# Squares and roots pinned to their written order on ScalarE around a pooling layer, and eps taken over a squared factor instead of a product after the root

## The chip, the cores and the metric

The kernel runs on one core of a Trainium2 chip. The metric is device time in microseconds (us), from launch to end, lower is better; the figure for the kernel before is the median of three runs. The engines are TensorE (PE), VectorE (DVE), ScalarE (ACT), GpSimd (POOL) and SyncE (SP, which issues the DMAs of weights).

## The reference, cut to what matters

512 tokens of width 1024 go through two blocks in float32. The second block has two layers. Layer 0 is attention and a SwiGLU FFN; layer 1 is a pooling mixer and a SwiGLU FFN. Every part is normed before and after:

```
rmsnorm(x, g) = x * rsqrt(mean(x*x) + eps) * g
h = h + rmsnorm(mixer(rmsnorm(h, g0)), g1)
h = h + rmsnorm(swiglu(rmsnorm(h, g2)), g3)
```

The pooling mixer takes, in four groups of 256 channels, the trailing mean over 2, 4, 8 or 16 tokens minus the token, a 256x256 map for each group, and a scale for each channel. `eps` is 1e-6.

## The kernel before, in words

Float32 products are made of three matmuls on operands split into a high part and a rest: weights `raw` come by DMA (512 KB each, from SP), ACT copies the high part `wh`, DVE subtracts for the rest `wl`. All tiles of this kind share one set of 37 buffers, so a load starts when a buffer comes free. The four token tiles of 128 are numbered 0 to 3; `XT[i]` is the residual of tile i, tokens on partitions, in two halves of 512 channels.

Operations go through a helper, so the trace gives all of them line 113. They are followed here by tile names.

**Norms.** The FFN's input is not normed before its matmuls. `Raw.put` (lines 1019 to 1026) transposes the plain residual and writes it, times the gain, to `H`; the tokens' factor `ra` = 1/sqrt(mean square + eps) is found beside it by `rstd_col` (999 to 1006) in `to_raw` (1072 to 1075), spread over partitions by PE and copied to `rsb` by ACT (`factors`, 1028 to 1031). The gate's output is multiplied by `rsb` ahead of SiLU. The up part is not multiplied, so the FFN's output lacks a factor `ra` for each token. The norm after it makes this good (`PostT.close`, 1061 to 1070): the root is taken of ss * ra*ra/D + eps, and its reciprocal is multiplied by `ra`. `factors` keeps ra*ra/D in `ra2` for that.

**The closing norm of a token tile.** `PostT.square` (1056 to 1059) squares each half `mg` on ACT with a sum over the row, and POOL multiplies the half by the gain. `close` adds the two sums on DVE (`sd`), takes the root on ACT (`sd`), the reciprocal on DVE (`rs`), and updates both halves of `XT` on DVE; then ACT squares both halves of `XT` for the next norm. In the second FFN `to_pool` (1708 to 1715) takes the next root and writes the scaled tokens `xs`, one half on ACT and one on DVE.

**Order of the work around the pooling layer** (1748 to 1784). `f2.last(h, j)` ends the FFN of layer 0 for two token tiles and one half of the channels; `band` multiplies `xs` by banded matrices, for two tiles at a time, and ACT and DVE write the result to `H`; `pool_step(i)` is the 256x256 maps of tile i, its closing norm and the `Raw.put` for the next FFN; `heads` are gate and up steps of an FFN on the first 256 tokens, written early so that PE has work. As written: `f2.last` for tiles 0 and 1, and the first half of the channels for tiles 2 and 3; the first band; pool steps 0 and 1; `f2.last` for tiles 2 and 3; two gate and up steps of the last FFN, whose evacuation is put off; the second band; the evacuation; pool steps 2 and 3; three more gate and up steps; the rest of the last FFN.

This is the order in which the code is written. The Tile framework schedules it: on each engine an instruction may be moved ahead of earlier ones that are not ready by its estimate. `keep` stops this for one instruction: it must come behind the instruction written just before it on its engine. In the kernel before, `keep` is on the roots of `rstd_col` and on the SiLUs put off. The squares have none. PSUM has four banks `mm`, two `ax` and two `st`; a gate and up step uses two of `mm`.

Of the kernel before, what the change touches and what calls it, by code (L numbers as in the profile page):

```python
# [11 lines left out]
AF = mybir.ActivationFunctionType  # L12
OP = mybir.AluOpType
# [5 lines left out]
D = 1024  # L19
# [12 lines left out]
EPS = 1e-6  # L32
# [88 lines left out]
def body(ctx: ExitStack, tc: tile.TileContext, I: dict, out, dbg=None):  # L121
# [12 lines left out]
    def A(name, dt=F32):  # L134
        tag, bufs = TAGS.get(name, ("m", NB))
        return ar.tile([P, 2, S], dt, tag=tag, name=name, bufs=bufs)
# [4 lines left out]
    def SQ():  # L141
        return tp.tile([P, S], F32, tag="sq", name="sq", bufs=BS)
# [4 lines left out]
    def small(w, name):  # L147
        return tp.tile([P, w], F32, tag=f"sm{w}", name=name, bufs=6)

    def MM():  # L150
        return ps.tile([P, S], F32, tag="mm", name="mm", bufs=4)
# [7 lines left out]
    def act(o, i, f=AF.Identity, **kw):  # L159
        ins = SC.activation(o, i, f, **kw)  # L160
        if f in KEEPF and not SC.on:
            tc.keep_in_program_order(ins)
        return ins

    def keep(ins):

        if KEEP:
            tc.keep_in_program_order(ins)

    def stt(o, a, s, b, op0, op1):  # L170
        return V.scalar_tensor_tensor(o, a, s, b, op0=op0, op1=op1)

    def tt(o, a, b, op):
        return V.tensor_tensor(o, a, b, op=op)

    def ts(o, a, s, op, s2=None, op2=None):
        if op2 is None:
            return V.tensor_scalar(o, a, s, None, op0=op)
        return V.tensor_scalar(o, a, s, s2, op0=op, op1=op2)
# [7 lines left out]
    def columns(name, w, t=None):  # L187

        if t is None:
            t = cp.tile([P, w], F32, name=name)  # L190
        used = [0]

        def f(n):
            used[0] += n
            return t[:, used[0] - n:used[0]]
        return f

    C = columns("fixed", 1576)

    ident, ones, blk = C(P), C(P), C(P)  # L200
    epsc = C(1)
# [33 lines left out]
    for i in range(4):  # L235
        a = A("xtok")
# [47 lines left out]
    class Weights:  # L284


        def __init__(self, look):
            self.look, self.deep = look, 1
            self.specs, self.loaded, self.ready, self.done = [], [], [], 0
            self.pool = False  # L290
            self.hp = 0
# [179 lines left out]
    def mm_tok(o, op, slabs, i, k0=0, first=True, last=True):  # L471
        lst = list(wk(slabs))
        ks_ = k0 if isinstance(k0, tuple) else range(k0, k0 + len(lst))
        for n, (k, (wh, wl)) in enumerate(zip(ks_, lst)):
            th, tl = op.tok(k, i)
            TE.matmul(o, lhsT=th, rhs=wh, start=(first and n == 0), stop=False)
            TE.matmul(o, lhsT=tl, rhs=wh, start=False, stop=False)
            TE.matmul(o, lhsT=th, rhs=wl, start=False, stop=(last and n == len(lst) - 1))
# [20 lines left out]
    def spread(rs, n, bank=ST):  # L499
        psb = bank()  # L500
        for i in range(n // P):
            TE.matmul(psb[:, i * P:(i + 1) * P], lhsT=rs[:, i:i + 1].to_broadcast([P, P]), rhs=ident, start=True, stop=True)
        return psb[:, :n]
# [454 lines left out]
    def heads(n, **kw):  # L958

        for _ in range(min(n, len(nx["head"]))):  # L960
            nx["head"].popleft()(**kw)

    def run(seq, n_of, step, close):

        left = {h: n_of for h in HALVES}
        cl = {}
        for m, c0, c1 in seq:
            step(m, c0, c1)
            for h in HALVES:
                if c0 <= h[0] and h[1] <= c1:  # L970
                    left[h] -= 1
                    if left[h] == 0:
                        cl[h] = close(*h)
                        if h == HALVES[0]:
                            next(cl[h])
                            next(cl[h])
                        else:
                            closing(cl[HALVES[0]], cl[h])
# [17 lines left out]
            return cache[m]  # L996
        return get

    def rstd_col(ss, out, ra=None):

        sd = small(4, "sd")
        tt(sd[:, :1], ss[:, 0:1], ss[:, 1:2], OP.add)
        keep(act(sd[:, 1:2], sd[:, :1], AF.Sqrt, scale=1.0 / D if ra is None else ra[1], bias=epsc))
        V.reciprocal(out, sd[:, 1:2])
        if ra is not None:
            tt(out, out, ra[0], OP.mult)

    XT = []

    class Raw:  # L1010


        def __init__(self, g, name):
            self.g = g
            self.ra = C(4)
            self.ra2 = C(4)
            self.rsb = tp.tile([P, S], F32, tag="rsb", name="rsb", bufs=1)

        def put(self, i):
# [8 lines left out]
        def factors(self, i):  # L1028
            a = self.ra[:, i:i + 1]
            act(self.rsb[:, i * P:(i + 1) * P], spread(a, P), AF.Copy)  # L1030
            stt(self.ra2[:, i:i + 1], a, 1.0 / D, a, OP.mult, OP.mult)

        def of(self, i):
            return self.ra[:, i:i + 1], self.ra2[:, i:i + 1]

    def row_of(src):

# [4 lines left out]
    class PostT:  # L1042
# [12 lines left out]

        def square(self, i, j):
            mv = self.m(i, j)
            act(SQ(), mv, AF.Square, accum_out=self.ss[:, i, j:j + 1])
            (G if TG[j] else V).tensor_tensor(mv, mv, self.gb[:, j], op=OP.mult)

        def close(self, i, last=False):
            rs = small(4, "rs")[:, :1]
            rstd_col(self.ss[:, i], rs, self.ra and self.ra.of(i))
            for j in range(2):
                x = XT[i][:, j]
                stt(x, self.m(i, j), rs, x, OP.mult, OP.add)
                if last:
                    nc.sync.dma_start(out[0, i * P:(i + 1) * P, j * S:(j + 1) * S], x)
                else:
                    act(SQ(), x, AF.Square, accum_out=self.ss[:, i, 2 + j:3 + j])  # L1070

        def to_raw(self, i):
            self.raw.put(i)
            rstd_col(self.ss[:, i, 2:], self.raw.ra[:, i:i + 1])
            self.raw.factors(i)

    posts = []

    def gate_up_step(op, hid, get, raw=None):
        def f(m, c0, c1, late=None):  # L1080
            n = c1 - c0
            sl = get(m)
            if hid.t[m] is None:
                hid.t[m] = A("hid", F32R)
            pg, pu = MM(), MM()
            mm_tile(pg[:, :n], op, sl[:1], c0, c1)
            mm_tile(pu[:, :n], op, sl[1:], c0, c1)

            def evac():
                t = T("silu")  # L1090
                if raw is None:
                    a = act(t[:, :n], pg[:, :n], AF.Silu)
                else:
                    tt(t[:, :n], pg[:, :n], raw.rsb[:, c0:c1], OP.mult)
                    a = act(t[:, :n], t[:, :n], AF.Silu)
                if late is not None or KEEPS:
                    keep(a)
                tt(t[:, :n], t[:, :n], pu[:, :n], OP.mult)
                hid.put(m, t[:, :n], c0, c1)
            if late is None:  # L1100
                evac()
            else:
                late.append(evac)
        return f
# [550 lines left out]
    def dump_tok(name):  # L1655
        if dbg is not None and name in dbg:
            for i in range(4):
                for k in range(KD):
                    nc.sync.dma_start(dbg[name][:, k, i * P:(i + 1) * P].rearrange("c t -> t c"), XT[i][:, k // 4, k % 4 * P:(k % 4 + 1) * P])
# [48 lines left out]
    def to_pool(i):  # L1708
        x_ = A("xs")
        xs.append(x_)  # L1710
        p = pf["p"]
        rs = small(4, "rs")[:, :1]
        rstd_col(p.ss[:, i, 2:], rs)
        act(x_[:, 0], XT[i][:, 0], AF.Copy, scale=rs)
        ts(x_[:, 1], XT[i][:, 1], rs, OP.mult)
# [19 lines left out]
    def pool_step(i):  # L1735
        psb, pp = pf["psb"], pf["pp"]
        for j in range(2):
            (wh, wl, _), = getp(j)
            o = MM()
            for e in range(2):  # L1740
                g = 2 * j + e
                mm_tok(o[:, e * HS:(e + 1) * HS], HO, [(wh[:, 2 * e:2 * e + 2], wl[:, 2 * e:2 * e + 2], 2)], i, 2 * g)
            tt(pp.m(i, j), o, psb[:, j], OP.mult)
            pp.square(i, j)
        pp.close(i)
        pp.to_raw(i)
# [10 lines left out]
    def after2(i):  # L1757
        f2.p.close(i)
        to_pool(i)
    f2.last(0, 0)  # L1760
    f2.last(0, 1, after2)
    f2.last(1, 0)
    band(*HALVES[0])
    pool_step(0)
    pool_step(1)
    f2.last(1, 1, after2)
    f3 = FfnT(HO, raw1, HEAD3)
    W.ahead(6)
# [7 lines left out]
        drain(e() for e in late)  # L1776
    pool_step(2)
    pool_step(3)
    heads(HEAD3)
    dump_tok("ha1")  # L1780
    f3.front(lambda: PostT(gnorm(1, 3), None, raw1))
# [24 lines left out]
```

## Time and profile before

| | us |
|---|---|
| median of 3 runs | 1663.76 |
| lowest, highest | 1662.12, 1664.29 |
| profiled execution | 1662.05 |
| its span, first to last instruction | 1660.3 |
| PE busy in the span | 1626.7 (98%) |
| DVE busy | 879.6 (53%) |
| ACT busy | 681.0 (41%) |
| POOL busy | 129.3 (8%) |

The span is what the trace covers; the time of an execution is a little more than its span. Times in the rows below are from the span's start. The pooling layer and the ends of its neighbours lie between about 1228 and 1330 us.

### The profile page before, as it was taken

What the parts mean: (1) busy time and instruction counts of PE and PEld (TensorE: products, weight loads), DVE (VectorE), ACT (ScalarE), POOL (GpSimd) and SP (SyncE); (2) the same over time, 40 slices, a digit from 0 to 9 for tenths busy, and PEclk for the clock granted to TensorE, in tenths of its full rate; (3) what the DMA queues carried; (4) which work ended last, traced back from release to release, by engine and by line L of the source; (5) the groups of instructions that cost most, each with busy time, mean ns of one, the idle gap of its engine ahead of it and who ended that gap; (6) DMA issues with size and microseconds to landing.
All of it is one profiled execution on the core that took longest, in us unless ns stands there. A gap on an engine that the chain in (4) does not pass through costs nothing.

```text
span 1660.3 us, 21934 instructions
## 1 busy us (share of the span) xinstructions
PE 1626.7 (98%) x8733; PEld 1355.0 (82%) x8733; DVE 879.6 (53%) x1644; ACT 681.0 (41%) x1231; POOL 129.3 (8%) x144
## 2 busy tenths in 40 slices
PE   7998999999999999999999999999998999999998
PEld 5886698888888998777778888888888998888886
DVE  4799583444433584778857344423257734432244
ACT  4585352322123455455658223313237823322232
POOL 0452000000000011101011000000022100000002
PEclk9999999999999999999999999999999999999999
DMA  9635434445452333301144133234221533232511
GB/s 306 180 113 209 161 99 117 136 132 173 146 139 80 95 79 79 90 26 52 39 134 108 51 101 89 83 107 140 77 89 54 138 89 102 75 108 92 144 38 51
DMA packets 245167, 179.53 MB, mean 108 GB/s; under 512 B 20688, under 2 KB 220224, under 8 KB 245064
## 3 DMA queue, kind: packets, MB, share of 16 engines
q1 hardware_dynamic: 240520, 176.99, 36.2%
q10 hardware_dynamic: 4544, 1.14, 0.4%
q8 instruction: 68, 1.11, 0.3%
q14 instruction: 35, 0.29, 0.1%
HBM read 175.99 MB, written 2.11 MB: 107 GB/s over the span
## 4 chain that ended last, share of the span: by engine, by line
PE 86%; DVE 4%; ACT 1%; issue 0%; DMA 0%; DVEq 0%; ACTq 0%
PE mm L113 80%; PE ax L113 3%; PE st L113 3%; DVE pw L113 1%; ACT sq L113 0%; DMA raw<-in_ffn_w_gate_dram 0%; DVE wl L113 0%; ACT pw L113 0%; DVE XT L113 0%; DVE H L113 0%; DVE sq L113 0%; DVE mg L113 0%; DVE pt L113 0%; DVE lg L113 0%; DVE fk L113 0%
## 5 line engine op out<-in xcount | busy, mean ns | idle before, releaser
L113 PE MATMUL mm<-H,wh 128*128 128x512 f32 (+1 forms) x3168 | 869.8, 360 | 7.4 <-ACT H L113 2.4
L113 PEld LDWEIGHTS mm<-H,wh 128*128 128x128 f32 x3168 | 563.7, 189 | 106.6 <-issue 8.7
L113 PE MATMUL mm<-H,wl 128*128 128x512 f32 (+1 forms) x1584 | 567.9, 359 | 0.0
L113 DVE TENSOR_TENSOR wl<-raw,wh 128x1024 fp32r<-128x1024 f32 (+1 forms) x257 | 309.7, 1218 | 232.9 <-ACT wh L113 219.8
L113 PEld LDWEIGHTS mm<-H,wl 128*128 128x128 f32 x1584 | 299.3, 189 | 46.8 <-issue 3.4
L113 ACT ACTIVATE wh<-raw 128x1024 fp32r<-128x1024 f32 (+1 forms) x257 | 261.4, 1040 | 132.6 <-PE mm L113 66.6
L113 PE MATMUL mm<-wh,hid 128*128 128x512 f32 x704 | 217.4, 389 | 0.0
L113 DVE TENSOR_TENSOR silu<-silu,mm 128x512 f32<-128x512 f32 (+1 forms) x77 | 47.0, 611 | 252.2 <-PE mm L113 248.2
L113 PEld LDWEIGHTS mm<-wh,hid 128*128 128x128 f32 x704 | 132.1, 188 | 27.1
L113 ACT ACTIVATE hid<-silu 128x512 fp32r<-128x512 f32 (+1 forms) x77 | 43.9, 570 | 254.7 <-DVE silu L113 254.7
L113 PE MATMUL mm<-wl,hid 128*128 128x512 f32 x352 | 137.3, 390 | 0.0
L113 PE MATMUL mm<-hid,wh 128*128 128x512 f32 (+1 forms) x464 | 117.1, 341 | 0.0
L113 PEld LDWEIGHTS mm<-hid,wh 128*128 128x128 f32 x464 | 80.2, 190 | 10.7 <-issue 1.2
L113 POOL TENSOR_TENSOR mg<-mg,gb 128x512 f32<-128x512 f32 x32 | 44.2, 1388 | 464.7 <-ACT sq L113 459.1
L113 ACT ACTIVATE silu<-silu 128x512 f32<-128x512 f32 (+1 forms) x52 | 29.3, 565 | 124.7 <-DVE silu L113 124.7
L113 PE MATMUL mm<-hid,wl 128*128 128x512 f32 (+1 forms) x232 | 79.0, 341 | 0.0
L113 PEld LDWEIGHTS mm<-wl,hid 128*128 128x128 f32 x352 | 66.1, 188 | 14.1 <-DVE wl L113 0.3
L113 DVE TENSOR_TENSOR silu<-mm,rsb 128x512 f32<-128x512 f32 (+1 forms) x52 | 31.6, 608 | 73.3 <-PE mm L113 72.6
L113 PE MATMUL mm<-wh,H 128*128 128x512 f32 (+2 forms) x256 | 66.0, 345 | 2.8 <-ACT wh L113 1.6
L113 DVE TENSOR_TENSOR hid<-silu,hid 128x512 fp32r<-128x512 f32 (+1 forms) x77 | 47.3, 614 | 32.5 <-ACT hid L113 32.5
L113 POOL TENSOR_TENSOR cv<-cv,tap 128x488 f32<-128x488 f32 (+12 forms) x40 | 52.5, 1345 | 88.1 <-ACT cv L113 71.1
L113 DVE SCALAR_TENSOR_TENSOR ax<-glu,fixed,ax 128x511 f32<-128x511 f32 (+21 forms) x76 | 51.4, 732 | 0.0
(271 smaller groups left out, 1582.8 us busy)
## 6 DMA issues: line engine op xcount, KB each, us to landing
adaw<-in_ada_w_dram SPq DMA_DIRECT2D x48, 512.0 KB
raw<-in_w_ffn_in_dram SPq DMA_DIRECT2D x44, 512.0 KB
raw<-in_ffn_w_gate_dram SPq DMA_DIRECT2D x44, 512.0 KB
raw<-in_ffn_w_up_dram SPq DMA_DIRECT2D x44, 512.0 KB
raw<-in_ffn_w_down_dram SPq DMA_DIRECT2D x44, 512.0 KB
raw<-in_w_in_dram SPq DMA_DIRECT2D x16, 512.0 KB
adaw<-in_ada_f_w_dram SPq DMA_DIRECT2D x16, 512.0 KB
raw<-in_attn_w_in_dram SPq DMA_DIRECT2D x16, 512.0 KB
```

The costliest lines, as they stand in the source:

```text
L113: ins = f(*a, **k)
```

## The change

The root of the closing norm now has `eps` / (ra*ra) as its bias and the constant 1/D as its scale: the factor `ra` cancels, and the product after the reciprocal goes. The earlier root `sd` is 1/ra, so `eps` times its square is computed in `to_raw` by one `scalar_tensor_tensor`, behind `factors`, which no longer computes `ra2`. This holds for both FFNs of the second block: eight closing norms, four token tiles each.

Between the second FFN's end and pool step 3 (`kept`), the squares in `PostT.square` and in `PostT.close` are kept in their written order as well.

```
--- before.py
+++ after.py
@@ -996,14 +996,13 @@
             return cache[m]
         return get
 
-    def rstd_col(ss, out, ra=None):
+    def rstd_col(ss, out, bias=None):
 
         sd = small(4, "sd")
         tt(sd[:, :1], ss[:, 0:1], ss[:, 1:2], OP.add)
-        keep(act(sd[:, 1:2], sd[:, :1], AF.Sqrt, scale=1.0 / D if ra is None else ra[1], bias=epsc))
+        keep(act(sd[:, 1:2], sd[:, :1], AF.Sqrt, scale=1.0 / D, bias=epsc if bias is None else bias))
         V.reciprocal(out, sd[:, 1:2])
-        if ra is not None:
-            tt(out, out, ra[0], OP.mult)
+        return sd[:, 1:2]
 
     XT = []
 
@@ -1013,7 +1012,7 @@
         def __init__(self, g, name):
             self.g = g
             self.ra = C(4)
-            self.ra2 = C(4)
+            self.eps = C(4)
             self.rsb = tp.tile([P, S], F32, tag="rsb", name="rsb", bufs=1)
 
         def put(self, i):
@@ -1028,10 +1027,9 @@
         def factors(self, i):
             a = self.ra[:, i:i + 1]
             act(self.rsb[:, i * P:(i + 1) * P], spread(a, P), AF.Copy)
-            stt(self.ra2[:, i:i + 1], a, 1.0 / D, a, OP.mult, OP.mult)
 
         def of(self, i):
-            return self.ra[:, i:i + 1], self.ra2[:, i:i + 1]
+            return self.eps[:, i:i + 1]
 
     def row_of(src):
 
@@ -1055,7 +1053,9 @@
 
         def square(self, i, j):
             mv = self.m(i, j)
-            act(SQ(), mv, AF.Square, accum_out=self.ss[:, i, j:j + 1])
+            a = act(SQ(), mv, AF.Square, accum_out=self.ss[:, i, j:j + 1])
+            if kept[0]:
+                keep(a)
             (G if TG[j] else V).tensor_tensor(mv, mv, self.gb[:, j], op=OP.mult)
 
         def close(self, i, last=False):
@@ -1067,14 +1067,18 @@
                 if last:
                     nc.sync.dma_start(out[0, i * P:(i + 1) * P, j * S:(j + 1) * S], x)
                 else:
-                    act(SQ(), x, AF.Square, accum_out=self.ss[:, i, 2 + j:3 + j])
+                    a = act(SQ(), x, AF.Square, accum_out=self.ss[:, i, 2 + j:3 + j])
+                    if kept[0]:
+                        keep(a)
 
         def to_raw(self, i):
             self.raw.put(i)
-            rstd_col(self.ss[:, i, 2:], self.raw.ra[:, i:i + 1])
+            sd = rstd_col(self.ss[:, i, 2:], self.raw.ra[:, i:i + 1])
             self.raw.factors(i)
+            stt(self.raw.eps[:, i:i + 1], sd, EPS, sd, OP.mult, OP.mult)
 
     posts = []
+    kept = [False]
 
     def gate_up_step(op, hid, get, raw=None):
         def f(m, c0, c1, late=None):
@@ -1757,6 +1761,7 @@
     def after2(i):
         f2.p.close(i)
         to_pool(i)
+    kept[0] = True
     f2.last(0, 0)
     f2.last(0, 1, after2)
     f2.last(1, 0)
@@ -1776,6 +1781,7 @@
         drain(e() for e in late)
     pool_step(2)
     pool_step(3)
+    kept[0] = False
     heads(HEAD3)
     dump_tok("ha1")
     f3.front(lambda: PostT(gnorm(1, 3), None, raw1))
```

## Rows read from the trace of the kernel before

**Rows 1.** The first line of the page.
```profile
span 1660.3 us, 21934 instructions
```

**Rows 2.** Busy time by stretch, from the pooling layer to the end; columns: the stretch in us from the span's start and its length, then for PE, PE's weight loads, DVE, ACT and POOL the busy us and the number of instructions, then TensorE's granted clock, the busy share of the DMA engines and GB/s.
```profile
1228.00:1248.40 20.40, 20.40 (x91) 16.60 (x90) 15.09 (x31) 10.50 (x21) 5.93 (x4) 1.00 0.29 90
1248.40:1266.00 17.60, 13.25 (x89) 11.63 (x88) 14.30 (x24) 12.11 (x28) 6.05 (x4) 1.00 0.44 120
1266.00:1300.00 34.00, 34.00 (x246) 32.14 (x245) 25.52 (x65) 25.67 (x68) 5.14 (x4) 1.00 0.39 102
1300.00:1326.00 26.00, 26.00 (x220) 25.91 (x219) 20.63 (x48) 24.67 (x54) 5.93 (x4) 1.00 0.35 91
1326.00:1648.00 322.00, 322.00 (x1509) 270.41 (x1508) 112.98 (x137) 88.85 (x122) 7.90 (x6) 1.00 0.29 87
1648.00:1660.30 12.30, 4.82 (x22) 3.65 (x20) 5.80 (x12) 2.22 (x6) 2.55 (x2) 0.89 0.22 85
```

**Rows 3.** PE's waits between 1225 and 1335 us; columns: who waited for whom, us in total, times, the longest.
```profile
PE ax L113 <- ACT xs L113: 2.0, 1, 2.0
PE ax L113 <- DVE XT L113: 1.1, 1, 1.1
PE mm L113 <- DVE H L113: 0.9, 1, 0.9
PE mm L113 <- ACT H L113: 0.3, 1, 0.3
```

**Rows 4.** ACT's instructions in order of time, 1237 to 1253 us, some of them; columns: start, duration in us, engine, line, operation, out<-in, count, and in brackets the idle time before and what ended it.
```profile
1237.94 0.63 ACT L113 ACTIVATE sq<-mg 128x512 f32<-128x512 f32 x1 [2.58 <-DVE mg L113]
...
1238.57 1.04 ACT L113 ACTIVATE wh<-raw 128x1024 fp32r<-128x1024 f32 x1
1239.63 1.28 ACT L113 ACT_TABLE_LOAD   x1
...
1244.16 0.62 ACT L113 ACTIVATE sq<-mg 128x512 f32<-128x512 f32 x1
...
1245.36 0.72 ACT L113 ACTIVATE xs<-XT,rs 128x512 f32<-128x512 f32 x1 [0.31 <-DVE rs L113]
...
1249.18 0.61 ACT L113 ACTIVATE sq<-mg 128x512 f32<-128x512 f32 x1
...
1250.40 0.28 ACT L113 ACTIVATE sd<-sd,fixed 128x1 f32<-128x1 f32 x1
...
1252.55 1.19 ACT L113 ACTIVATE H<-ax,fixed 128x256 fp32r<-128x256 f32 x3
```

**Rows 5.** The same view of ACT, 1260 to 1286 us.
```profile
1260.77 0.63 ACT L113 ACTIVATE sq<-mg 128x512 f32<-128x512 f32 x1 [1.03 <-DVE mg L113]
...
1267.32 0.63 ACT L113 ACTIVATE sq<-mg 128x512 f32<-128x512 f32 x1
...
1268.43 0.65 ACT L113 ACTIVATE sq<-mg 128x512 f32<-128x512 f32 x1
...
1269.55 0.32 ACT L113 ACTIVATE sd<-sd,fixed 128x1 f32<-128x1 f32 x1
...
1272.05 0.28 ACT L113 ACTIVATE rsb<-st 128x128 f32<-128x128 f32 x1 [1.40 <-PE st L113]
...
1274.27 0.64 ACT L113 ACTIVATE sq<-mg 128x512 f32<-128x512 f32 x1
...
1279.82 0.62 ACT L113 ACTIVATE sq<-mg 128x512 f32<-128x512 f32 x1
...
1285.70 0.73 ACT L113 ACTIVATE xs<-XT,rs 128x512 f32<-128x512 f32 x1 [0.23 <-DVE rs L113]
```

**Rows 6.** DVE's instructions in order of time, two of them: the update of the residual of token tile 1 in the second FFN, and the sum of two squares of the first pool step.
```profile
1247.10 1.42 DVE L113 SCALAR_TENSOR_TENSOR XT<-mg,rs,XT 128x512 f32<-128x512 f32 x2
...
1262.47 1.25 DVE L113 TENSOR_TENSOR sd<-fixed 128x1 f32<-128x1 f32 x1
```

**Rows 7.** PE's instructions in order of time: the start of the second half's banded matmuls.
```profile
1286.87 4.46 PE L113 MATMUL ax<-bm,xs 128*128 128x256 f32 x30
```

**Rows 8.** ACT's instructions in order of time, 1305 to 1311 us.
```profile
1305.79 1.28 ACT L113 ACT_TABLE_LOAD   x1
1307.08 0.42 ACT L113 ACTIVATE silu<-silu 128x256 f32<-128x256 f32 x1
...
1309.13 0.62 ACT L113 ACTIVATE sq<-mg 128x512 f32<-128x512 f32 x1
...
1310.61 0.62 ACT L113 ACTIVATE sq<-mg 128x512 f32<-128x512 f32 x1
```

**Rows 9.** All engines in order of time, the end of the kernel: the last token tile's norm.
```profile
1654.50 0.16 DVE L113 TENSOR_TENSOR sd<-fixed 128x1 f32<-128x1 f32 x1 [0.79 <-ACT sq L113]
1654.55 1.26 POOL L113 TENSOR_TENSOR mg<-mg,gb 128x512 f32<-128x512 f32 x1 [2.96 <-ACT sq L113]
...
1655.31 0.51 DVE L113 TENSOR_TENSOR rs<-rs,fixed 128x1 f32<-128x1 f32 x1
1655.86 1.42 DVE L113 SCALAR_TENSOR_TENSOR XT<-mg,rs,XT 128x512 f32<-128x512 f32 x2
```

**Rows 10.** The DMA queue's own waits between 1225 and 1335 us, columns as in group 3.
```profile
SPq L309 <- ACT sq L113: 14.3, 1, 14.3
```

**Rows 11.** DMA issues of SP in order of time: the first weight load after 1226.3 us.
```profile
1250.52 0.37 SPq L309 DMA_DIRECT2D raw<-in_ffn_w_up_dram  x1
```

More of the change, by code (lines that the diff above doesn't have):

```diff
@@ L997, in lazy, with rstd_col @@
         return get
-    def rstd_col(ss, out, ra=None):
+    def rstd_col(ss, out, bias=None):
         sd = small(4, "sd")
         tt(sd[:, :1], ss[:, 0:1], ss[:, 1:2], OP.add)
-        keep(act(sd[:, 1:2], sd[:, :1], AF.Sqrt, scale=1.0 / D if ra is None else ra[1], bias=epsc))
+        keep(act(sd[:, 1:2], sd[:, :1], AF.Sqrt, scale=1.0 / D, bias=epsc if bias is None else bias))
         V.reciprocal(out, sd[:, 1:2])
-        if ra is not None:
-            tt(out, out, ra[0], OP.mult)
+        return sd[:, 1:2]
     XT = []
@@ L1015, in __init__ @@
             self.ra = C(4)
-            self.ra2 = C(4)
+            self.eps = C(4)
             self.rsb = tp.tile([P, S], F32, tag="rsb", name="rsb", bufs=1)
@@ L1030, in factors @@
             act(self.rsb[:, i * P:(i + 1) * P], spread(a, P), AF.Copy)
-            stt(self.ra2[:, i:i + 1], a, 1.0 / D, a, OP.mult, OP.mult)
         def of(self, i):
-            return self.ra[:, i:i + 1], self.ra2[:, i:i + 1]
+            return self.eps[:, i:i + 1]
     def row_of(src):
@@ L1057, in square @@
             mv = self.m(i, j)
-            act(SQ(), mv, AF.Square, accum_out=self.ss[:, i, j:j + 1])
+            a = act(SQ(), mv, AF.Square, accum_out=self.ss[:, i, j:j + 1])
+            if kept[0]:
+                keep(a)
             (G if TG[j] else V).tensor_tensor(mv, mv, self.gb[:, j], op=OP.mult)
@@ L1069, in close @@
                 else:
-                    act(SQ(), x, AF.Square, accum_out=self.ss[:, i, 2 + j:3 + j])
+                    a = act(SQ(), x, AF.Square, accum_out=self.ss[:, i, 2 + j:3 + j])
+                    if kept[0]:
+                        keep(a)
         def to_raw(self, i):
             self.raw.put(i)
-            rstd_col(self.ss[:, i, 2:], self.raw.ra[:, i:i + 1])
+            sd = rstd_col(self.ss[:, i, 2:], self.raw.ra[:, i:i + 1])
             self.raw.factors(i)
+            stt(self.raw.eps[:, i:i + 1], sd, EPS, sd, OP.mult, OP.mult)
     posts = []
+    kept = [False]
     def gate_up_step(op, hid, get, raw=None):
@@ L1759, in after2 @@
         to_pool(i)
+    kept[0] = True
     f2.last(0, 0)
@@ L1778, in body @@
     pool_step(3)
+    kept[0] = False
     heads(HEAD3)
```

## The prediction

> **What bounds the kernel now.** I read the page first, then busy time by stretch, then TensorE's waits in the stretch around the pooling layer, then the order of the instructions on ScalarE (ACT), VectorE (DVE) and GpSimd (POOL) there, and last the end of the kernel. The span is 1660.3 us [rows 1]. TensorE (PE) is the bound: it is busy in every microsecond from 1266 to 1648, with a granted clock of 1.00 (the 2.4 GHz level) [rows 2]. Around the pooling layer it is idle in one stretch alone, 17.60 - 13.25 = 4.35 us between 1248.4 and 1266 [rows 2], in four waits: 2.0 for the scaled tokens `xs`, 1.1 for `XT`, 0.9 and 0.3 for `H` [rows 3]. After the last matmuls 7.5 us of the last 12.3 are idle on PE [rows 2]: that is the closing norm and the stores. So nothing the change does can win more than some 4.4 us in the pooling layer and a little at the end. A loss has no such lid: every chain on ACT that grows past the matmuls which cover it is a new wait of PE.
>
> The cover is thin. The scaled copy `xs` of the last token tile starts at 1285.70 and takes 0.73, so it is there at 1286.43; the banded matmuls that read it start at 1286.87 [rows 5, 7]. That is 0.44 us of slack, and it decides this case.
>
> **What the change does, part by part.**
>
> *Formula.* Before, `eps` stayed inside the root and the product of the root's reciprocal with the tokens' factor came after it, one 128x1 product per closing norm, eight in all. Now the root's bias carries `eps` times the square of the earlier root, and there is no product. One 128x1 `scalar_tensor_tensor` for each token tile goes and one comes: nothing. The four products of the last FFN stand at the end of the kernel, the last of them on the path: it starts at 1655.31 and takes 0.51 us, though the 128x1 sum at 1654.50 took 0.16. Its end, 1655.82, is the end of the POOL product with the gain (1654.55 + 1.26 = 1655.81), and the update of `XT` starts at 1655.86 [rows 9]. The second half of that update reads the product, and the first reads two tensors of SBUF like the 128x1 product that was held. So the stall passes from the product to the update: what is late next is POOL. I take 0; at most the product's whole 0.51 comes back. The other four products, 0.2 us each with the gap behind them, are inside the chains below.
>
> *Pins.* Each square and each root of the stretch is put behind the ACT instruction written before it. Before, only the roots were. No instruction is added; the order changes in three places.
>
> *(a) Second FFN, tokens 0 and 1.* The square of tile 1 ran at 1244.16, ahead of tile 0's second root and of its `xs` at 1245.36 [rows 4]; written, it comes after that `xs`. Tile 0's root need not wait for it and its first update need not wait for the product, so I put the end of that `xs` 0.45 earlier, near 1245.65. There tile 1's square starts, 1.5 later than before, and ends near 1246.4. POOL's product behind it takes 1.3 us, as at the end of the kernel [rows 9], to 1247.75, and holds the update of `XT`, which took 1.42 from 1247.10 [rows 6] and now ends near 1249.15 instead of 1248.52. From there to tile 1's second root it was 1.88 us, of which 1.22 were the squares of tiles 2 and 3 that ran ahead of it, at 1249.18 to 1250.40 [rows 4]. Those now come after its `xs`, but a square of `XT` and a sum remain, 1.1 us: the root comes near 1250.3, 0.1 earlier, and the 2.0 us wait for `xs` [rows 3] nearly stays. The two squares, 1.2 us, then stand ahead of the `H` copies that started at 1252.55 [rows 4], for which PE already waits 0.3 and 0.9 us [rows 3]. Between -1.2 (all of the 1.22 won) and +1.2 (the copies late by the squares) I take +0.3. A queue hangs on it too: SP waited 14.3 us for an ACT square and issued a weight load at 1250.52, just behind these squares [rows 10, 11]. If it is the moved square that frees the buffer, that load and the three behind it are 2.4 us late; this I leave to the range, as the trace doesn't say what is freed.
>
> *(b) Pool steps 0 and 1, then tokens 2 and 3 of the FFN.* Here two token tiles ran overlapped on ACT, and this is where the pins cost. Step 1's squares ran at 1267.32 and 1268.43, in the middle of step 0's `H` copies; the FFN's square of tile 2 ran at 1274.27, in the middle of step 1's; that of tile 3 at 1279.82, before tile 2's `xs` (all [rows 5]). Written, step 1's squares come after step 0's factor copy `rsb`, tile 2's square after step 1's `rsb`, and tile 3's after tile 2's `xs`. Each is the head of a chain (square, sum, root, reciprocal, update, square, sum, root, reciprocal, copy), so four chains now run end to end:
> - Step 0 took from 1260.77 to `rsb` at 1272.05; without step 1's squares and root between (0.63 + 0.65 + 0.32 = 1.6) `rsb` starts at 1270.45: 9.7 us [rows 5].
> - Step 1 begins 0.2 later and takes 9.7 again, less 0.6: step 0's sum took 1.25 us [rows 6] where 0.16 is its own time, and I count half of that excess as not to be met again. 1270.65 + 9.1 = 1279.75.
> - A token tile of the FFN: tile 0 went from its square at 1237.94 to the end of `xs` at 1246.08, 8.14 us. Less a table load 1.28, a weight copy 1.04 and the other tile's square 0.62 [rows 4]: 5.2. Less the product 0.2; plus 0.5, as POOL's product (1.3 us, running from the square's end) now ends after sum, root and reciprocal (0.8). 5.5, and 11.0 for two.
> - 1279.75 + 0.2 + 11.0 = 1290.95 for the last `xs`, against PE's arrival at 1286.87 [rows 7]: a new wait of 4.1 us.
>
> PE has nothing to put there: all four `mm` banks are held by the two gate and up steps whose evacuation is written after the band. If each of the four chains is 0.5 shorter than its row the wait is 2.1; if each is 0.5 longer, 6.1. I take 4.1.
>
> *(c) Pool steps 2 and 3.* Step 3's squares ran at 1309.13 and 1310.61, before step 2's second root [rows 8]. Pinned, they come after step 2's `rsb`, near 1314, so `H` of step 3 begins some 2.5 us later than before. PE covers this with the three remaining gate and up steps, and for those that follow, all reading that `H`, it can start on two of them at once. I take +1.0; between 0 and +3 (a wait of the whole 2.5 and another load). ACT is busy 24.67 of the 26 us there [rows 2], so it has no gaps to give. A switch between SiLU and root costs here the load alone: it starts at 1305.79, takes 1.28, and SiLU starts at 1307.08 [rows 8].
>
> The Trainium skill (ScalarE: Activation LUTs, What ACT_TABLE_LOAD costs) puts each switch at about 2.66 us, with a drain of 1.38 beside the load. By that figure the bound of (c) would be +4.4 instead of +3; the row shows no drain, and the sum goes by the row.
>
> **Sum.** 0.3 + 4.1 + 1.0 + 0 = +5.4 us. The profiled execution took 1662.05, 1.75 over its span; the median of the runs is 1663.76, 1.71 over that. So 1662.05 + 5.4 = 1667.45 for such an execution, and 1663.76 + 5.4 = **1669.2** as the median.
>
> **Rivals.** A difference of 0.2% (3.3 us) is about what can be told from no change.
>
> *The chains get shorter than their rows, and the slack holds.* With fewer strangers on ACT the copies of `H` may run faster, and PE may put the band's cover elsewhere. It decides at 1286.87: if the four chains take 26.1 us from 1260.77 instead of 30.2, there is no new wait. Then (a) may give its 1.2 and the end its 0.5: 1663.76 - 1.7 = 1662.1, not slower. For it: the reordering was worth something only where ACT was the limit, and it had gaps. Against it: the latencies of sum, root and update don't shrink with less work on ACT. Chance 0.28.
>
> *The idle of the first stretch goes.* If POOL's product holds up the update of tile 1 less than I think, and the `H` copies come in order, up to 2.0 + 1.1 + 0.9 + 0.3 vanish [rows 3], with 0.5 at the end: 1663.76 - 4.8 = 1659.0. It needs (b) to cost nothing besides. Chance 0.08.
>
> *It doesn't do what it says.* A pin binds a square only to the instruction before it; if that one was already early, the order stays. For the squares of (b) the one before is `rsb`, which was late, so I doubt it. 1663.8, chance 0.07.
>
> *More than one queue gets later.* The loads behind the moved square come 2.4 us late, and (c) has its 3: 5.4 + 2.4 + 2.0, about 1673.5. Chance 0.09.
>
> My forecast: 0.48. Its own range is 1666.5 to 1671.5, from the bounds of (b) and (c).
>
> **How the numbers follow.** Slower by over 0.2% means above 1667.1: the worse case 0.09 and nearly all of the forecast, 0.46, so 0.55. Faster means below 1660.4: 0.08. The rest, 0.37, is the first and third rival and the forecast's low edge. The range runs from 1661.5, which leaves out the second rival and little of the first, to 1672.5, which leaves out the worst.
>
> **What would show it.** Right: step 1's first square after the first `rsb`, the last `xs` near 1291, and a PE wait of some 4 us for `xs` at the second band; the first wait for `xs` still near 2 us; the 128x1 product gone at the end and `XT` still starting as POOL ends. Wrong: no wait at the second band, or the last `xs` at or before 1287.

## The result, and the profile after

The changed kernel takes 1681.65 us (median of 6 runs, 1674.55 to 1682.27) against 1663.53 for the kernel before on the same chip: a ratio of 1.0103 [1.0092, 1.0115], some 17 to 18 us slower. The prediction had the direction (slower, 0.55) and the place (waits of TensorE around the pooling layer); 1669.2 was too low and the range, which ended at 1672.5, did not hold it. The profiled execution took 1682.27, the slowest of the six, and the profiled one before took 1662.05, quicker than any of its six; so the two traces are 20.2 us apart where the medians are 18.1 apart.

The page of the changed kernel, span and busy time:

```profile
span 1680.5 us, 21917 instructions
...
PE 1635.9 (97%) x8733; PEld 1362.9 (81%) x8733; DVE 882.5 (53%) x1636; ACT 682.7 (41%) x1231; POOL 129.5 (8%) x144
```

The same line of the kernel before:

```profile
PE 1626.7 (98%) x8733; PEld 1355.0 (82%) x8733; DVE 879.6 (53%) x1644; ACT 681.0 (41%) x1231; POOL 129.3 (8%) x144
```

The span is 20.2 us longer than the one in [rows 1]. PE runs the same 8733 matmuls, but is busy 9.2 us longer with them; the other 11.0 us are idle time. Both halves need a cause; this difference of 20.2 us is the loss that the text below explains. The waits of PE between 1225 and 1350 us, after (columns as in [rows 3]):

```profile
PE ax L113 <- DVE XT L113: 9.9, 3, 4.9
PE ax L113 <- ACT xs L113: 4.7, 2, 2.4
```

That is 14.6 us against 4.3 in [rows 3]. Where they stand, from PE's instructions in order of time (start, duration, operation, count, in brackets the wait ahead of it and for whom):

```profile
1252.93 1.48 PE L113 MATMUL ax<-bm,xs 128*128 128x128 f32 x6 [2.38 <-ACT xs L113]
...
1269.39 0.63 PE L113 MATMUL ax<-fixed,XT 128*128 128x128 f32 x4 [1.73 <-DVE XT L113]
...
1279.20 1.45 PE L113 MATMUL ax<-fixed,XT 128*128 128x128 f32 x8 [3.23 <-DVE XT L113]
1280.34 1.17 PE L113 MATMUL mm<-H,wh 128*128 128x256 f32 x4
...
1297.47 2.74 PE L113 MATMUL ax<-bm,xs 128*128 128x128 f32 x12 [2.36 <-ACT xs L113]
...
1335.77 1.94 PE L113 MATMUL ax<-fixed,XT 128*128 128x128 f32 x8 [4.95 <-DVE XT L113]
```

In order: the first band's `xs`, the transposes of pool steps 0 and 1 (`XT`), the second band's `xs`, and the transposes of pool step 3. The prediction had a new wait at one of these places, the second band. Busy time by stretches of 4 us shows the other half (columns as in [rows 2]; the last three numbers are granted clock, DMA share and GB/s):

```profile
1252.00:1256.00 4.00, 3.06 (x11) 2.62 (x12) 1.76 (x4) 3.94 (x9) 2.50 (x2) 0.64 0.15 40
1256.00:1260.00 4.00, 4.00 (x29) 3.78 (x28) 3.84 (x6) 2.90 (x7) 0.00 (x0) 0.94 0.81 222
...
1280.00:1284.00 4.00, 4.00 (x22) 4.00 (x23) 2.55 (x9) 3.20 (x11) 0.00 (x0) 0.57 0.00 0
1284.00:1288.00 4.00, 4.00 (x36) 4.00 (x35) 1.02 (x7) 1.18 (x4) 0.74 (x1) 1.00 0.02 4
...
1296.00:1300.00 4.00, 2.52 (x12) 2.53 (x13) 2.39 (x6) 2.91 (x5) 0.00 (x0) 0.68 0.91 248
1300.00:1304.00 4.00, 4.00 (x16) 3.64 (x16) 2.51 (x5) 2.01 (x4) 0.00 (x0) 0.50 0.59 146
1304.00:1308.00 4.00, 4.00 (x30) 3.78 (x30) 2.70 (x5) 2.76 (x6) 0.00 (x0) 0.96 0.99 271
...
1336.00:1340.00 4.00, 4.00 (x18) 3.68 (x18) 3.40 (x10) 3.32 (x12) 0.00 (x0) 0.50 0.00 0
1340.00:1344.00 4.00, 4.00 (x29) 4.00 (x28) 1.08 (x5) 1.05 (x4) 0.00 (x0) 0.77 0.00 0
```

Behind four of the five waits the granted clock falls to or towards 0.50, the 1.2 GHz level, and a full stretch then holds 16 to 18 matmuls (of mixed shapes) where at 1.00 it holds up to 36. The kernel before has 1.00 in every stretch from 1228 to 1648 [rows 2]. With busy time times (1 - clock) as the price of the fall, the loss by place, in us, is:

| place | wait after | wait before | lower clock |
|---|---|---|---|
| first band, `xs` | 2.4 | 2.0, and 1.2 for `H` behind it | 1.3 |
| pool step 0, transposes | 1.7 | 1.1 | 0 |
| pool step 1, transposes | 3.2 | 0 | 1.7 |
| second band, `xs` | 2.4 | 0 | 3.0 |
| pool step 3, transposes | 5.0 | 0 | 2.9 |
| sum | 14.6 | 4.3 | 8.9 |

10.3 of waits and 8.9 of clock are 19.2 of the 20.2. Of the rest, 1.1 is idle time of PE in the first 100 us (busy 87.32 against 88.46), before any of the code that the pins touch; the end gives 0.3 back.

Two chains behind these waits. ACT of the changed kernel, pool step 0's root to the last `xs`, some rows:

```profile
1267.37 0.29 ACT L113 ACTIVATE sd<-sd,fixed 128x1 f32<-128x1 f32 x1 [2.63 <-DVE sd L113]
...
1275.15 0.28 ACT L113 ACTIVATE rsb<-st 128x128 f32<-128x128 f32 x1 [0.91 <-PE st L113]
1275.32 0.62 ACT L113 ACTIVATE sq<-mg 128x512 f32<-128x512 f32 x1
...
1286.29 0.28 ACT L113 ACTIVATE rsb<-st 128x128 f32<-128x128 f32 x1 [2.36 <-PE st L113]
1286.47 0.62 ACT L113 ACTIVATE sq<-mg 128x512 f32<-128x512 f32 x1
...
1296.70 0.72 ACT L113 ACTIVATE xs<-XT,rs 128x512 f32<-128x512 f32 x1 [0.23 <-DVE rs L113]
```

The pins do what the prediction said: step 1's square stands right behind step 0's `rsb`, tile 2's behind step 1's, and ACT waits inside each chain instead of working on the next. And ACT in pool steps 2 and 3, after:

```profile
1327.01 1.28 ACT L113 ACT_TABLE_LOAD   x1
1328.30 0.29 ACT L113 ACTIVATE sd<-sd,fixed 128x1 f32<-128x1 f32 x1
...
1329.76 0.26 ACT L113 ACTIVATE rsb<-st 128x128 f32<-128x128 f32 x1
1329.91 0.62 ACT L113 ACTIVATE sq<-mg 128x512 f32<-128x512 f32 x1
...
1331.26 1.28 ACT L113 ACT_TABLE_LOAD   x1
1332.55 0.42 ACT L113 ACTIVATE silu<-silu 128x256 f32<-128x256 f32 x1
1332.98 1.28 ACT L113 ACT_TABLE_LOAD   x1
1334.28 0.29 ACT L113 ACTIVATE sd<-sd,fixed 128x1 f32<-128x1 f32 x1
```

against the same place before:

```profile
1311.85 1.28 ACT L113 ACT_TABLE_LOAD   x1
1313.15 0.29 ACT L113 ACTIVATE sd<-sd,fixed 128x1 f32<-128x1 f32 x1
1313.85 0.29 ACT L113 ACTIVATE sd<-sd,fixed 128x1 f32<-128x1 f32 x1
```

Before, step 2's second root and step 3's first stood side by side behind one load. Pinned, step 3's squares come after step 2's `rsb`, so its root comes 5.98 us behind step 2's and not 0.70; a SiLU has slipped between, and its two loads and itself (1.28 + 0.42 + 1.28 = 3.0) stand in step 3's chain.

The end of the kernel, after, as [rows 9]:

```profile
1675.00 0.16 DVE L113 TENSOR_TENSOR sd<-fixed 128x1 f32<-128x1 f32 x1 [0.79 <-ACT sq L113]
1675.04 1.26 POOL L113 TENSOR_TENSOR mg<-mg,gb 128x512 f32<-128x512 f32 x1 [2.79 <-ACT sq L113]
...
1675.52 0.16 DVE L113 RECIPROCAL rs<-sd 128x1 f32<-128x1 f32 x1 [0.36 <-ACT sd L113]
1675.72 1.80 DVE L113 SCALAR_TENSOR_TENSOR XT<-mg,rs,XT 128x512 f32<-128x512 f32 x2
```

The product is gone. From the sum's start to the end of both updates it is 2.52 us instead of 2.78 [rows 9]: 0.26 won. The pair starts 0.58 before POOL's product ends (1675.04 + 1.26 = 1676.30), but takes 1.80 instead of 1.42: its second half needs that product.

### The profile page after: what moved, and what is told of

It is laid out like the page before. It is cut to its first block, busy times and chain, and to the rows that moved or that the text cites. A ratio compares the mean times of both kernels' runs of the same rounds, so it can differ in the third digit from the quotient of the medians.

```text
span 1680.5 us, 21917 instructions
## 1 busy us (share of the span) xinstructions
PE 1635.9 (97%) x8733; PEld 1362.9 (81%) x8733; DVE 882.5 (53%) x1636; ACT 682.7 (41%) x1231; POOL 129.5 (8%) x144
## 5 line engine op out<-in xcount | busy, mean ns | idle before, releaser
L113 PEld LDWEIGHTS mm<-hid,wh 128*128 128x128 f32 x464 | 80.2, 190 | 10.6 <-issue 1.2
```

The source lines that it names most:

```text
L113: ins = f(*a, **k)
```

## Experiments

The theories, in words (letters in the expectations name them as they stood when each was written): the loss is the waits alone, at their own length; a good half of it is the clock that falls behind them; the loads of ACT's table lengthen the last part; the parts of the pinned stretch lengthen one chain together. All ratios are to the kernel before. The flag `kept` switches the pins; a diff is cut to what matters and is against the changed kernel, where the flag is set ahead of `f2.last(0, 0)` and cleared behind `pool_step(3)`. Where a diff sets the flag elsewhere, the first setting is gone. "The formula alone" below is the kernel with the new formula and no pins; the other losses are read against it. A difference between two ratios is known to about 0.0014, some 2 us.

**The formula alone.**

```
-    kept[0] = True        # never set
```

> The new formula without any pinned square. Theory A (the pins are the whole loss): within 0.2% of the kernel before, 1660 to 1667 us, TensorE idle for no more than some 4.5 us between 1228 and 1340 us and its granted clock 1.00 there. Theory B (the formula moves the schedule, and that costs): 1672 us or more, with new waits in the same stretch. Of my prediction it tests the term 0 for the formula.

1660.26 us, 0.9987 [0.9977, 0.9997]: 2.2 us faster (0.5 to 3.8), where the prediction took 0. PE's waits are 3.4 us instead of 4.3 and the end gives its 0.26, 1.2 in all; the rest is inside the interval. So the loss comes from the pins.

**The pins alone**: the kernel before, with the squares pinned as in the change and the product as it was.

```
-        sd = rstd_col(...); ...; stt(self.raw.eps[:, i:i + 1], sd, EPS, sd, OP.mult, OP.mult)
+        rstd_col(...)         # product and scale as before
     kept[0] = True
```

> The pinned squares with the old formula. Theory A: nearly all of the loss, 1677 to 1685 us, with some 14 us of TensorE waits in the pooling layer and a granted clock near 0.9 there. Theory B: 1667 us or less.

1677.38 us, 1.0091 [1.0068, 1.0114], with much the same waits: `XT` 8.8 us in three (longest 4.9), `xs` 5.5 in two, `H` 0.6. The pins don't need the new formula to cost what they cost.

**Pins before the first band only.**

```
     band(*HALVES[0])          # kept[0] = False ahead of it
```

> The new formula, squares pinned only in the end of the second FFN for the first half of its work (before the first band). Theory A (late loads): the pinned squares of tokens 2 and 3 hold the weight loads back by 2 to 3 us, a weight split then stands ahead of pool step 0's sum, the wait of TensorE for xs grows from 1.3 to 2.4 us, that for XT stays near 1.7 to 2, and the clock falls behind the longer wait: 1663 to 1668 us. Rival (only the xs chain, my prediction's step (a), +0.3, at most +1.2): 1660 to 1662, loads where they were or without effect.

1663.04 us, 0.9997 [0.9987, 1.0006]. The wait for `xs` is 2.38 us, as in the changed kernel, and the one at step 0's transposes 1.73. The weight load that stood at 1250.74 with the formula alone is issued at 1253.39: the queue that the prediction left to its range does come 2.6 us late. This part of the pins, with that queue, costs little by itself.

**Pins of the two squares of tiles 2 and 3 only** (second FFN, first column half).

```
+    kept[0] = True
     f2.last(1, 0)
+    kept[0] = False
```

> The new formula, with only the two squares of the second FFN's tokens 2 and 3 in the first half of the channels pinned behind the scaled copy of tile 1. If the square ahead of the root is what the first wait for xs is made of, that wait falls from 1.3 to about 0.7 us: 1659 to 1660.5, 0.2% under the kernel before. If the moved squares hold loads back or stand ahead of the H copies: 1661 to 1665.

1659.40 us (11 runs), 0.9982 [0.9973, 0.9991], the fastest of all here and faster than both kernels, though its interval overlaps that of the formula alone. The root of tile 1 no longer waits for a square of another tile: the wait for `xs` falls to 0.82 us. That these two squares stood ahead of tile 1's root, the prediction's (a) read rightly; in the changed kernel the wait is 2.38 again with the pins of tiles 0 and 1 added. That this kernel is faster than the formula alone isn't shown.

**Pins of the middle only** (pool steps 0 and 1, tokens 2 and 3).

```
+    kept[0] = True
     pool_step(0)
     pool_step(1)
     f2.last(1, 1, after2)
+    kept[0] = False
```

> The new formula, squares pinned only from pool step 0 to the second FFN's last token tiles. Theory A: the waits of TensorE for XT (1.7 and 3.2 us in the changed kernel) and for the last xs (2.4) and two falls of the clock behind them; without the first part's and the last part's waits: 1670 to 1677 us. My prediction's step (b) as it stood (one wait of 4.1 us at the second band, clock unchanged): 1667 to 1669. If only all the pins together make the loss: 1666 or less.

1664.90 us, 1.0014 [1.0004, 1.0024], so 0.0027 above the formula alone, some 4.5 us. This is the prediction's (b) by itself. Its last `xs` starts at 1290.41 and ends at 1291.13, where 1290.95 was forecast for the end. But the wait at the second band is 1.64, and another stands at step 1's transposes. PE of this kernel:

```profile
1264.71 0.63 PE L113 MATMUL ax<-fixed,XT 128*128 128x128 f32 x4 [1.14 <-DVE XT L113]
...
1274.09 1.32 PE L113 MATMUL ax<-fixed,XT 128*128 128x128 f32 x8 [0.99 <-DVE XT L113]
...
1291.18 1.51 PE L113 MATMUL ax<-bm,xs 128*128 128x128 f32 x12 [1.64 <-ACT xs L113]
```

The granted clock is 1.00 in every stretch here. The end of the chain was forecast well; what PE does meanwhile was not. PE's waits between 1225 and 1350 us are 5.7 us, 2.3 more than with the formula alone; the rest of the 4.5 is not in this trace, and is about what the two ratios leave open.

**Pins of pool step 1's squares only.**

```
+    kept[0] = True
     pool_step(1)
+    kept[0] = False
```

> The new formula, only pool step 1's squares pinned behind step 0's factor copy. If the prediction's chain holds (step 1 starting 3 us later delays the last xs past TensorE's arrival): a wait for xs at the second band of 1 to 3 us, 1661.5 to 1665. If the room in ACT makes up for it: no such wait, 1659 to 1661.

1663.57 us, 1.0010 [1.0001, 1.0020]. The wait at step 1's transposes is 0.99 again, and there is none at the second band, against what was expected. Of the 0.0023 above the formula alone, some 3.8 us, the trace shows about 1.1 as waits (4.5 against 3.4); the rest isn't explained, beyond what the two ratios leave open.

**Pins of pool steps 2 and 3 only.**

```
+    kept[0] = True
     pool_step(2)
     pool_step(3)
```

> The new formula, squares pinned only in pool steps 2 and 3. Theory A: the wait of 5 us for XT behind the three gate and up steps and the fall of the clock after it, 1668 to 1673 us. My prediction's step (c) as it stood (+1, at most +3, clock unchanged): 1664 to 1666.5. If the wait there only follows from the delays before it: 1664 or less.

1668.45 us, 1.0032 [1.0023, 1.0042], so 0.0045 above the formula alone, some 7.5 us, for the part priced at +1.0. PE waits 4.46 us at step 3's transposes, with the same two loads and SiLU in the chain, and the clock falls behind it:

```profile
1316.00:1320.00 4.00, 0.10 (x1) 0.00 (x0) 1.55 (x4) 3.58 (x10) 2.48 (x2) 0.87 0.31 92
1320.00:1324.00 4.00, 3.44 (x14) 3.05 (x15) 3.67 (x8) 3.61 (x11) 0.00 (x0) 0.50 0.00 0
```

**The same without the table loads**, and its control without pins. Both leave out the SiLU of five gate and up steps, so they compute something else; only their times are read.

```
-                    a = act(t[:, :n], t[:, :n], AF.Silu)
+                    a = act(t[:, :n], t[:, :n], AF.Copy if raw is raw1_[0] and n < S and c0 == 0 else AF.Silu)
```

> The kernel with squares pinned only in pool steps 2 and 3, and the SiLU of the last FFN's first five gate and up steps on the first 256 tokens replaced by a copy: these leave out the SiLU, so no table is loaded between roots and SiLUs there. To be read against the next kernel. Theory E (the pins cost in steps 2 and 3 because two more table loads of 1.28 us and a SiLU stand in the chain from step 2's root to step 3's): TensorE's wait for XT of 4.5 us falls to some 1 to 2, and the time is within 3 us of the next kernel. Theory F (the chain in written order is too long by itself): the wait stays above 3 us and the time stays 5 to 9 us above the next kernel.

> The new formula without pins, with the same five SiLUs left out and copied instead: the control for the kernel above. TensorE is busy throughout that part already, so both theories expect the time of the formula alone, 1658 to 1662 us.

With pins 1662.00 us, 1.0000 [0.9991, 1.0010]; without, 1661.96, 0.9999 [0.9990, 1.0008]. Once no SiLU stands near, the pins of steps 2 and 3 cost nothing that can be told (0.0001). ACT of the kernel with pins, the same place:

```profile
1310.29 0.28 ACT L113 ACTIVATE sd<-sd,fixed 128x1 f32<-128x1 f32 x1
...
1314.03 0.29 ACT L113 ACTIVATE sd<-sd,fixed 128x1 f32<-128x1 f32 x1 [0.47 <-DVE sd L113]
```

The two roots are 3.74 us apart where with the loads they were 4.72 (1314.44 and 1319.16), PE waits 0.96 at step 3's transposes, and the clock stays at 1.00. That the control is not faster than the formula alone (0.9999 against 0.9987, overlapping intervals) is not explained.

**Work for PE in the waits**: the changed kernel, and eleven 128x512 matmuls whose result nobody reads, placed where PE would wait.

```
+    def fill(n, dep, rhs):
+        o = ST()
+        for k in range(n):
+            TE.matmul(o, lhsT=dep.to_broadcast([P, P]), rhs=rhs, start=True, stop=True)
...
+            if kept[0] and i in (1, 3):      # in to_raw
+                fill(3 if i == 1 else 4, self.ss[:, i, 0:1], self.gb[:, 0])
...
+        if i in (1, 3):                      # in to_pool
+            fill(2, p.ss[:, i, 2:3], p.gb[:, 0])
```

> The changed kernel with eleven extra matmuls (128x512, written to a PSUM bank that nobody reads) put where TensorE waits: 2 before xs of tile 1, 3 before the transposes of pool step 1, 2 before xs of tile 3, 4 before the transposes of pool step 3. They add work and take no wait away from the chains. Theory C (half of the loss is the clock, which falls behind a wait of TensorE): the granted clock stays near 1.00 between 1248 and 1348 us and the time falls by 5 to 9 us against the changed kernel, to 1672 to 1677. Theory D (the clock falls for another reason, or the extra busy time is the order of the matmuls): the clock stays near 0.9 there and the time is that of the changed kernel or up to 4 us above, 1680 to 1686.

1673.90 us, 1.0066 [1.0052, 1.0081]: work was added and the kernel became some 6 us faster than the changed one (0.0037, by the ratios). The trace has each added matmul as two, 22 in all. The page, and stretches of it that answer to those of the changed kernel:

```profile
PE 1637.5 (98%) x8755; PEld 1357.8 (81%) x8755; DVE 881.1 (53%) x1636; ACT 681.6 (41%) x1231; POOL 129.6 (8%) x144
```

```profile
1266.00:1300.00 34.00, 31.76 (x199) 26.62 (x200) 22.55 (x55) 22.22 (x61) 5.07 (x4) 1.00 0.19 49
...
1326.00:1348.00 22.00, 20.41 (x157) 18.73 (x156) 11.32 (x26) 12.53 (x27) 0.67 (x1) 1.00 0.23 68
```

The added matmuls are busy 10.5 us; without them PE's busy time is 1627.0, that of the kernel before (1626.7). The clock is 1.00 in every stretch of 4 us from 1244 to 1352. So the 9.2 us of longer matmuls were the clock, and not the order of the matmuls. The waits have not gone: fill and remaining idle time are 15.5 us together.

**First and middle pins, without the last.**

```
     f2.last(1, 1, after2)
+    kept[0] = False
```

> The new formula, squares pinned in the first and the middle part together, not in pool steps 2 and 3. Theory G (the late weight loads of the first part lengthen the middle's chains): the waits for XT are those of the changed kernel, 1.7 and 3.2 us, not 1.1 and 1.0 as with the middle part alone, and the time is 1670 to 1676 us, more than the two parts' own losses together (about 0.1 and 0.27% over the formula alone: 1666.5). If the parts add up: 1665 to 1668, with waits as in the middle part alone.

1674.07 us, 1.0070 [1.0055, 1.0085]. Above the formula alone, the first part costs 0.0010 and the middle 0.0027, but together 0.0083: they don't add. PE:

```profile
1276.91 1.97 PE L113 MATMUL ax<-fixed,XT 128*128 128x128 f32 x8 [3.23 <-DVE XT L113]
```

The wait at step 1's transposes has grown from 0.99 to 3.23, and the clock falls behind it (0.50 in 1276 to 1280, 0.69 in 1280 to 1284).

**The two squares and the middle.** What joins them: the weight loads that the first pins make late, or slack that both use?

```
+    kept[0] = True
     f2.last(1, 0)
+    kept[0] = False
     band(*HALVES[0])
+    kept[0] = True
     pool_step(0)
     pool_step(1)
     f2.last(1, 1, after2)
+    kept[0] = False
```

> The formula, the pins of the middle (pool steps 0 and 1, tokens 2 and 3) and, of those before the first band, only the two squares of tiles 2 and 3 (the edit that alone gave 0.9982). TensorE's order is that of first plus middle. What is read: between the last matmul of pool step 1's product and the gate and up steps, which read both token tiles' H, PE has only the 37 matmuls of the second FFN's last down projection; two chains (step 0, step 1) have to fit beside them. If the chains do it, each of the edits alone uses slack that exists once, so they don't add here either: the wait for XT at step 1's transposes is 2.5 to 3.5 us as in first plus middle (3.23), only the first wait for xs is shorter (0.8 instead of 2.4), the wait for xs at the second band stays near 2, the granted clock falls after both, and the ratio is 1.0045 to 1.0065. If instead the weight loads that came 2.6 us late joined the two parts (here they are issued 1 us late at most), the wait at step 1's transposes is about 1, as with the middle pins alone (0.99), and the ratio is the sum of the two edits, 1.0000 to 1.0015.

1669.94 us, 1.0040 [1.0026, 1.0054]. The wait at step 1's transposes is 3.23 here too:

```profile
1275.34 1.84 PE L113 MATMUL ax<-fixed,XT 128*128 128x128 f32 x8 [3.23 <-DVE XT L113]
...
1293.62 1.51 PE L113 MATMUL ax<-bm,xs 128*128 128x128 f32 x12 [2.37 <-ACT xs L113]
```

So of the first pins it is the two squares that join with the middle; those of tiles 0 and 1, which made the first wait 2.38, are not needed for it. Between the squares and the load that they hold back this run doesn't decide. The load is issued at 1252.20, where with first and middle pins it was 1253.79, but all that stands around it is 1.6 us earlier as well: in both kernels it comes 1.10 us behind the start of the first band's waiting matmuls (1251.10 and 1252.69), and with the middle pins alone 0.73 ahead of it (1250.92 and 1251.65). The trace does show how the parts meet. From the last down projection's first matmul to step 1's transposes it is 13.64 us, 2.03 more than with the middle pins alone. Step 0's first square comes 1.37 us ahead of that matmul instead of 2.64, and its chain up to `rsb` takes 10.95 instead of 10.15. The time is a little under what was expected (1.0045 to 1.0065): in the profiled execution, at 1667.13, the clock fell behind the 3.23 alone (0.57 in 1276 to 1280), not behind the 2.37. The five runs lie at 1667.0 and 1667.1, with a mean granted clock of 0.995, and at 1669.9 to 1670.8, with 0.993 to 0.994; that one more fall is the 3 us between them is likely, not shown. In the changed kernel it is alike: 1674.55 at 0.994, the other five 1680.9 to 1682.3 at 0.990 or 0.991.

## Why the prediction was right and wrong

**What PE has for cover, step (b).** Here the prediction failed first. It counted everything PE did between 1266 and 1286.87 as cover for four chains in a row, and put the price where that ends. But the gate and up steps ahead of the second band read the columns of `HALVES[0]`, that is of token tiles 0 and 1: they can't start before pool step 1's transposes. From the end of the pool steps' maps until then PE has little but step 0's transposes and the last down projection of the second FFN, 36 matmuls. In the changed kernel step 1's transposes start 1279.20 - 1264.52 = 14.7 us after that projection's first matmul, of which 1.73 + 3.23 are waits: 9.7 us of work. Before, it was 1272.26 - 1263.41 = 8.9 us, and 8 of these matmuls ran after those transposes, 1.9 us: that was the slack. The pins of the middle make the stretch 11.6 us long (with one matmul left), those of the first part 10.6 (two left), the two together 13.6 (none). Each alone mostly uses the slack; together they pay. From step 1's transposes on, the second cover (the gate and up steps) starts late as well, so PE comes later to the second band: 1295.11 instead of 1286.87. Its wait there is 2.36, not 4.1, though the last `xs` ends at 1297.42, 6.5 us behind the forecast's 1290.95. That delay is 2.2 from the late start of step 0, 2.5 from its longer chain, 1.8 from step 1 and -0.1 from the two token tiles. With the middle pins alone it ends at 1291.13, 0.2 off, and that is partly luck: the chains began 0.9 us earlier than in the row used and took 1.1 us longer than the 30.2. That this part alone costs some 4.5 us where 4.1 was priced is luck as well: its trace has waits of 0.99 and 1.64 at two places, not one of 4.1.

**Step 0's chain.** It was put at 9.7 us from its first square to `rsb` and takes 12.2 (1262.99 to 1275.15). Of the 2.5, 0.5 is there with the middle pins alone (10.15) and 0.8 more with the two squares as well (10.95; 10.94 with first and middle pins). The last 1.2 isn't the pins': the kernel of first and middle pins has the same ones up to this place and doesn't show it. DVE has a weight copy in front of step 0's sum in every kernel, and here it began behind POOL's product (one row of POOL, then two of DVE):

```profile
1263.79 3.52 POOL L113 TENSOR_TENSOR mg<-mg,gb 128x512 f32<-128x512 f32 x2 [7.82 <-ACT sq L113]
...
1263.89 2.28 DVE L113 TENSOR_TENSOR wl<-raw,wh 128x1024 fp32r<-128x1024 f32 x1
1266.10 1.24 DVE L113 TENSOR_TENSOR sd<-fixed 128x1 f32<-128x1 f32 x1
```

The copy took 2.28 us where others of its kind take 1.2. It did so in three of the fourteen traces (2.28 with the pins before the first band, 2.15 with the formula alone), just those whose clock fell behind the first band; in them it starts 0.1 to 0.2 us behind POOL's product. In the other eleven it starts 0.05 to 0.23 us ahead of that product and takes 1.21 or 1.22. So this piece goes with the clock, as far as fourteen traces tell. The queue named in the prediction, with the load behind the moved squares, does come late (1254.03 instead of 1250.52 [rows 11]) but doesn't make the copy slow: with the formula alone the load is on time (1250.74) and the copy slow, with first and middle pins it is late (1253.79) and the copy takes 1.21.

**Pool steps 2 and 3, step (c).** The mechanism was there (a later square, another load); the size was off. +1.0 was taken and 3 was the bound, though what it names, 2.5 and a load of 1.28, adds up to 3.8; the wait is 4.95 after, 4.46 with these pins alone. Counted were one load and a delay of 2.5 us; there are two loads and a SiLU, as the two tiles' roots no longer share one. On the price of a switch, the row [rows 8] and not the 2.66 us that the Trainium skill gives (ScalarE: Activation LUTs, What ACT_TABLE_LOAD costs) was again right: after, the load takes 1.28 and the SiLU starts 0.01 later.

**The clock.** The sum held every matmul at its duration of before, so it put a fall of the clock at 0 without a reason, and 8.9 of the 20.2 us are that. Around the pooling layer nothing showed what a longer wait does: the 2.00 us one passed at 1.00. But the start of the same trace of before did, at a wait of 2.35 us:

```profile
23.49 1.58 PE L113 MATMUL mm<-H,wh 128*128 128x512 f32 x2 [2.35 <-ACT H L113]
```

```profile
24.00:28.00 4.00, 4.00 (x20) 2.09 (x22) 3.25 (x4) 2.00 (x3) 0.00 (x0) 0.50 1.09 348
28.00:32.00 4.00, 4.00 (x35) 2.50 (x28) 0.56 (x4) 0.77 (x2) 0.00 (x0) 0.81 1.09 348
```

Priced as above that is 4.00 x 0.50 + 4.00 x 0.19 = 2.8 us behind one wait. Put into the sum, with the waits as measured at step 1's transposes and the second band (3.2 + 2.4 for 4.1) and at step 3 (5.0 for 1.0), the clock brings the forecast to 5.4 + 8.9 + 1.5 + 4.0 = 19.8 of the 20.2. By size the clock was the largest miss, then step (c), then step (b).

**Step (a)** was right in its main row: the wait for `xs` is 2.38, forecast "near 2". The 1.2 us of waits for `H` behind it are gone, and the clock behind it costs 1.3. **The formula** was put at 0, at most 0.5 at the end. The end gives 0.26; alone it is 2.2 us faster, more than the end explains.

**What was asked of the profile**: step 1's square behind `rsb`, yes; a wait for `xs` at the second band, yes, 2.36; the last `xs` near 1291, no, 1297; the product gone, yes; `XT` starting as POOL ends, no, its first half starts before. Of the rivals the one with a later queue and a dearer (c) came nearest in number, at 1673.5 and 0.09; that the later loads cost anything is not shown, and it lacked the clock as well.

Not tried: another place for step 1's transposes in PE's order, or more work that doesn't read them ahead of them; nor the two squares pinned with the load left where it was. What makes the clock fall behind one wait and not behind another stays open.

## What to carry to other kernels

Cover is not the time until the next wait in the profile, but the work that doesn't itself read what the chain makes: ask for each matmul counted as cover whose output it reads, and count what was left over behind the last one as the only slack. Where a pin makes two overlapped chains run end to end, look for what they shared (here one table load for two roots), as it may be paid twice. A new wait of a busy TensorE costs its length and, where the clock falls behind it, here 0.5 to 1.3 times as much again (1.7 behind 3.2, 3.0 behind 2.4); look through the whole trace of before for such a pair before pricing it at nothing. Unread matmuls put into the waits got some 6 of the 8.9 us back here.

## What the hardware showed that was not expected

Waits of some microseconds were followed by a granted clock between 0.50 and 0.81 in one or two of the 4 us stretches behind them, and that cost 1.3 to 3.0 us beside waits of 2.4 to 5.0. The length of a wait alone does not decide: the 2.00 us before [rows 3] and the 1.64 with the middle pins passed with a clock of 1.00. The same wait in two profiled executions went both ways: 1.29 at the first band was followed by 0.66 in 1252 to 1256 with the formula alone and by 1.00 with the middle pins, 2.38 there by 0.64 in the changed kernel and by 1.00 with first and middle pins, and 2.37 at the second band by 0.52 with first and middle pins and by 1.00 with the two squares and the middle. A weight copy on DVE took 2.15 to 2.28 us where it started up to 0.22 us behind POOL's product, and 1.22 where it started up to 0.23 us ahead of it. And unread matmuls made a kernel faster: 10.5 us of them took 6 us off.
